# Second chunk of the gated convolution input, DFT tables of the channels and first transfers in a two-layer encoder kernel on one Trainium2 core

## The chip, the core and the metric

The kernel runs on one core of a Trainium2 chip. TensorE (PE) multiplies matrices, VectorE (DVE), ScalarE (ACT) and GpSimd (POOL) work on tiles of 128 partitions, SyncE (SP) issues most transfers between the chip's memory and the core's. Each engine works through its own list of instructions in order and waits on semaphores for the others. The metric is the device time of one execution in microseconds; less is better. The time of the kernel before is 1168.14 us, the median of three runs (1167.82 to 1168.42).

## The reference

A trunk of two layers is applied with the same weights to a prompt of 512 positions and to a sample of 1024, both of width 1024, in fp32.

```
even layer:  h = rms_norm(x);  p = h @ w_in
             a_val, a_glu, f_in, a_z, f_z = split(p, five times 512)
             a = a_val * sigmoid(a_glu)
             a = depthwise conv of width 31 (a) + b
             a = silu(layer_norm(a)) * silu(a_z)
             f = Re(DFT over positions and over the 128 channels of each of 4 groups)(f_in)
             f = (f @ w_four per group) * silu(f_z)
             x = x + concat(a, f) @ w_out
odd layer:   u, b, c, z = split(rms_norm(x) @ w_in, four times 1024)
             x = x + (b * conv of width 3 (c * u) * silu(z)) @ w_out
output:      rms_norm(x)
```

## The kernel before

Activations are kept transposed: a tile has 128 channels on the partitions and a chunk of 512 positions along the free axis. The prompt, Q in the code, is one chunk; the sample, S, is two. A projection makes one output tile of 128 channels and 512 positions in PSUM. Its precision comes from splitting: each weight half and each activation is cast to fp32r (`hi`) on ScalarE, and the remainder (`lo`) is taken by a subtraction on VectorE or GpSimd. A projection then is three times eight matmuls over the eight tiles k of the width: `hi*hi`, `hi*lo`, `lo*hi` (`project`, line 175). In the trace the activations are `nh` and `nl` (normed), `rh` and `rl` (the prompt's, normed late), the weights `wo`, or `wp` where they lie in other buffers.

`load_w` (line 152) brings two halves of 256 KB through SP's queue into four raw buffers `wf`, casts them on ScalarE and subtracts on GpSimd. Weight tiles go to four buffers `wo`, or into a named pool: `load_w(..., "F")` takes four of the 16 buffers `F`, which also hold the inputs `x` of a chunk, eight tiles, and the tables `tb` of the position DFT, split into `tbh` and `tbl`.

The norm of a sample chunk (`norm_in`, `norm_in_rest`) sums squares, has PE transpose the sum (`cs`), computes the reciprocal root with a Newton iteration on GpSimd (`y`, line 214), makes a diagonal `d` on ScalarE (line 223) and spreads it with a matmul by ones (`r`, line 262). Then VectorE multiplies each of the eight `x` by `r`, ScalarE casts `nh`, and VectorE, for two of the eight GpSimd, subtracts `nl`.

The program is written out in order at lines 1130 to 1212; a scheduler then moves instructions of each engine by a timeline of its own, within the data dependences. The even layer's first part runs: the prompt's gated values (`l1_glu(Q)`), its Fourier input, the sample's first norm, the prompt's Fourier transform, its gates, the sample's second norm, then the sample's gated values `l1_glu(S, skew=True)`. For each of four channel tiles j that function makes the gate `glu` (sigmoid, tile `sig`) and the value `val` on both chunks and multiplies them into `a`. For j = 0 the order is gate and value on chunk 0, then `between`, which is the prompt's last Fourier gate `fz` with its weights in `F`, then gate and value on chunk 1. For j = 1 to 3 the gate runs on both chunks, then the value.

`fourier_tables` (line 446) loads and splits the position tables and multiplies the channel DFT `cdft` with the four group matrices `wf4`: two fp32 matmuls `wcs`, for the prompt and again, with another scale, for the sample. Beside all this VectorE runs the convolutions of width 31 (`conv31`, line 567), 30 taps of a multiply and add for each channel tile: `cv`, 128x512 for the prompt, 128x1024 for the sample.

The first lines of the program issue the small parameters `par_sb` and the constants `cst_sb` on ScalarE's queue, and the prompt's `x` and the first weights on SP's.

Of the kernel before, what the change touches and what calls it, by code (L numbers as in the profile page):

```python
# [11 lines left out]
AF = mybir.ActivationFunctionType  # L12
# [4 lines left out]
P = 128  # L17
# [46 lines left out]
def encoder(ctx: ExitStack, tc: tile.TileContext, xp, xs, w1, w1o, w2, w2o, wf4, par, cst, cdft, dft, outp, outs):  # L64
    nc = tc.nc
# [278 lines left out]
    def l1_glu(seq, h, skew=False, w0=None, between=None):  # L344
        for j in range(4):
            if seq is S:
                a = dp("a", seq.T + 2 * HALO)
            else:
                a = pool.tile([P, seq.T + 2 * HALO], F32, name=nm("ap"), tag="ap", bufs=4)
            nc.vector.memset(a[:, 0:HALO], 0.0)  # L350
            nc.vector.memset(a[:, HALO + seq.T:], 0.0)
            sig = [None] * seq.nc

            def do_glu(c, pq=None):
                if pq is None:
                    pq = project("glu", wg, h[c])
                t = sig[c] = pg("T", "sig")
                act_scaled(seq, t, pq, AF.Sigmoid)
                if seq.r is not None:
                    tt(t, t, seq.r, ALU.mult)  # L360

            def do_val(c, pq=None):
                if pq is None:
                    pq = project("val", wv, h[c])
                tt(a[:, HALO + c * CH:HALO + (c + 1) * CH], pq, sig[c], ALU.mult)

            if j == 0 and w0 is not None:
                pg_, pv_ = project_pair(w0, h[0])
                do_glu(0, pg_)
                do_val(0, pv_)  # L370
                seq.a.append(a)
                continue
            wg = load_w(w1, 4 + j)
            if skew and j == 0:
                wv = load_w(w1, j)
                for c in range(seq.nc):
                    do_glu(c)
                    do_val(c)
                    if c == 0 and between:
                        between()  # L380
            else:
                for c in range(seq.nc):
                    do_glu(c)
                wv = load_w(w1, j)
                for c in range(seq.nc):
                    do_val(c)
            seq.a.append(a)
# [51 lines left out]
    def azs(seq, h, c, js, n):  # L439
# [3 lines left out]
            l1_az(seq, h, c, [j])  # L443
        yield 1

    def fourier_tables(seq):
        seq.tab = {}
        for part in range(seq.parts):
            for q in range(2):
                t = ld("tb", dft[2 * part + q])  # L450
                seq.tab[q, part] = split(t, "F", "tb")
        wf4_sb = ld("w4", wf4)
        base = 0 if seq is S else 2 * P
        chan_dft = ld("cd", cdft)
        seq.wcs = []
        for q in range(2):
            pw = ps_st("wcs")
            nc.tensor.matmul(pw, chan_dft[:, base + q * P:base + (q + 1) * P], wf4_sb, start=True, stop=True)
            t = pg("T", "wcs")
            nc.scalar.copy(t, pw)  # L460
            seq.wcs.append(t)

    def fourier(seq):
# [663 lines left out]
        return t  # L1127


    nc.scalar.dma_start(par_sb, par)  # L1130
    xq = load_x(Q, 0, range(0, 1))
    w0 = load_w_pair(w1, 4, 0, lambda: xq.extend(load_x(Q, 0, range(1, 4))))
    xq += load_x(Q, 0, range(4, KD))
    one = pg("T", "one")
    nc.vector.memset(one, 1.0)
    nc.vector.tensor_copy(ones_r, one[:, 0:P])
    nc.vector.tensor_scalar(out=lnmean, in0=one[:, 0:P], scalar1=1.0 / 512.0, scalar2=None, op0=ALU.mult)
    nc.scalar.dma_start(cst_sb, cst)
    hq, hi_i, lo_i = norm_late(Q, xq)
    hq = [hq]  # L1140
    norm_late_r(Q, xq, hi_i, lo_i)
# [54 lines left out]
    at, seq = [], []  # L1196
# [80 lines left out]
```

## Time and profile before

| what | value |
|---|---|
| median of the runs | 1168.14 us |
| profiled execution, its own time | 1167.41 us |
| its span, first to last instruction | 1165.6 us |
| mean granted clock of TensorE | 0.991 |
| PE busy | 1135.6 us, 97% |
| DVE busy | 864.1 us, 74% |
| ACT busy | 470.9 us, 40% |
| POOL busy | 539.3 us, 46% |

Times in the trace are microseconds from the span's start. A row of a timeline gives start, duration, engine, line, operation, tiles, shape and count, and in brackets the idle time of the engine just before, with what ended it. The ends of matmuls are modelled and overlap; the starts are the measure of pace. A row of waits gives the waiting instruction and what it waited for, the sum in us, the number of times and the longest.

### The profile page before, as it was taken

The numbers are of one execution on the slowest core, as the hardware profiler recorded it, in microseconds if no ns is written. First come the engines' busy times: TensorE is split into PE (matmuls) and PEld (weight loads), VectorE is DVE, ScalarE is ACT, GpSimd is POOL, SyncE is SP. The second block draws the span as 40 slices with busy tenths as digits, with TensorE's granted clock in tenths as the row PEclk, the third lists the DMA queues.
The fourth block names the chain that finished last, engine by engine and source line by source line (L and its number), as shares of the span: only waits on it lengthen the run. The fifth ranks groups of instructions, "written<-read, shape, count | busy, mean of one in ns | idle before, by whom it ended". The sixth has DMA issues, their size and how long they took to land. (4 is left out here: it accounts for less than half of the span.)

```text
span 1165.6 us, 15047 instructions
## 1 busy us (share of the span) xinstructions
PE 1135.6 (97%) x5208; PEld 936.4 (80%) x5208; DVE 864.1 (74%) x1202; ACT 470.9 (40%) x823; POOL 539.3 (46%) x448
## 2 busy tenths in 40 slices
PE   7999989999999999999999999999999999999995
PEld 6778868888888888887778887878888888888895
DVE  5899988999899995678775799886464546554565
ACT  6543552233233344445433544442433333343431
POOL 3453632222246565544645454645545454444551
PEclk9999999999999999999999999999999999999998
DMA  9423312111234656535634758644222122034853
GB/s 325 138 91 95 104 46 64 55 37 55 82 97 153 205 190 223 172 99 183 192 123 145 283 191 297 224 157 142 89 75 79 58 82 82 28 106 141 281 173 123
DMA packets 89212, 159.63 MB, mean 137 GB/s; under 512 B 9904, under 2 KB 13488, under 8 KB 89136
## 3 DMA queue, kind: packets, MB, share of 16 engines
q1 hardware_dynamic: 88848, 158.37, 41.2%
q8 instruction: 41, 0.67, 0.2%
q14 instruction: 35, 0.29, 0.1%
q10 hardware_dynamic: 288, 0.30, 0.1%
HBM read 127.96 MB, written 30.67 MB: 136 GB/s over the span
## 5 line engine op out<-in xcount | busy, mean ns | idle before, releaser
L146 POOL TENSOR_TENSOR wo<-wf,wo 128x512 fp32r<-128x512 f32 x272 | 377.8, 1406 | 447.6 <-ACT wo L145 330.9
L145 ACT CAST wo<-wf 128x512 fp32r<-128x512 f32 x274 | 160.4, 618 | 217.1 <-PE X L742 37.3
L146 POOL TENSOR_TENSOR wo<-as,wo 128x512 fp32r<-128x512 f32 x80 | 111.3, 1391 | 112.6 <-ACT wo L145 108.1
L564 DVE SCALAR_TENSOR_TENSOR cv<-a,par_sb,cv 128x1024 f32<-128x1024 f32 x120 | 154.3, 1286 | 6.9 <-ACT cv L562 4.6
L189 PE MATMUL one<-ysh,wo 128*128 128x512 f32 x432 | 110.1, 392 | 0.7 <-ACT wo L145 0.4
L145 ACT CAST wo<-as 128x512 fp32r<-128x512 f32 x80 | 49.7, 621 | 140.3 <-PE X L742 86.5
L189 PE MATMUL one<-nh,wo 128*128 128x512 f32 x384 | 93.9, 391 | 2.4 <-ACT wo L145 2.4
L189 PEld LDWEIGHTS one<-ysh,wo 128*128 128x128 f32 x432 | 80.6, 188 | 18.6 <-ACT wo L145 0.9
L110 DVE TENSOR_TENSOR acc<-acc,sq 128x512 f32<-128x512 f32 (+1 forms) x77 | 76.3, 999 | 23.2 <-ACT sq L281 22.5
L564 DVE SCALAR_TENSOR_TENSOR cv<-ap,par_sb,cv 128x512 f32<-128x512 f32 x120 | 90.2, 752 | 2.6
L189 PEld LDWEIGHTS one<-nh,wo 128*128 128x128 f32 x384 | 71.8, 188 | 18.3 <-ACT wo L145 3.2
L742 PE MATMUL X<-bsh,wo 128*128 128x512 f32 x256 | 84.6, 391 | 0.0
L189 PE MATMUL one<-ysl,wo 128*128 128x512 f32 x216 | 58.3, 390 | 0.7 <-DVE ysl L110 0.7
L742 PEld LDWEIGHTS X<-bsh,wo 128*128 128x128 f32 x256 | 48.1, 188 | 10.6
L742 PE MATMUL X<-bsl,wo 128*128 128x512 f32 x128 | 50.1, 391 | 0.0
L189 PE MATMUL one<-nl,wo 128*128 128x512 f32 x192 | 49.3, 392 | 0.0
L189 PEld LDWEIGHTS one<-ysl,wo 128*128 128x128 f32 x216 | 40.5, 188 | 9.9 <-DVE ysl L110 1.1
L110 DVE TENSOR_TENSOR mc<-Z,mc 128x512 f32<-128x512 f32 x16 | 11.1, 691 | 46.9 <-PE Z L742 46.9
L742 PE MATMUL Z<-bsh,wo 128*128 128x512 f32 x128 | 44.3, 389 | 0.0
L742 PE MATMUL X<-ysh,wo 128*128 128x512 f32 x128 | 42.7, 398 | 0.1
L742 PE MATMUL Y<-bh,wo 128*128 128x512 f32 x128 | 42.4, 392 | 0.0
L189 PEld LDWEIGHTS one<-nl,wo 128*128 128x128 f32 x192 | 36.0, 188 | 7.9 <-issue 0.5
(314 smaller groups left out, 2476.3 us busy)
## 6 DMA issues: line engine op xcount, KB each, us to landing
wf<-w SPq DMA_DIRECT2D x224, 256.0 KB, 2.9
wf<-w2o SPq DMA_DIRECT2D x48, 256.0 KB, 3.5
wf<-w1o SPq DMA_DIRECT2D x32, 256.0 KB, 3.1
x1d<-xr SPq DMA_DIRECT2D x24, 256.0 KB, 2.1
x1r<-x1d SPq DMA_DIRECT2D x24, 256.0 KB, 4.0
xr<-x1d SPq DMA_DIRECT2D x19, 256.0 KB, 4.4
x<-xs SPq DMA_DIRECT2D x16, 256.0 KB, 5.3
y<-y SPq DMA_DIRECT2D x16, 256.0 KB, 4.0
```

The lines of the kernel that those rows point to most:

```text
L110: ins = eng.tensor_tensor(out=out, in0=a, in1=b, op=op)
L145: nc.scalar.copy(hi, t)
L146: eng.tensor_tensor(out=lo, in0=t, in1=hi.bitcast(F32), op=ALU.subtract)
L189: nc.tensor.matmul(out[:, 0:width], a[k], act[k][b][:, cols], start=(n == 0), stop=(n == 3 * KD - 1))
L564: nc.vector.scalar_tensor_tensor(out=acc, in0=src[:, t:t + n], scalar=col(w0 + t), in1=acc, op0=ALU.mult, op1=ALU.add)
L742: nc.tensor.matmul(out, self.w[p][a][:, k * P:(k + 1) * P], self.ops[p][k][b], start=(first and n == 0), stop=(n == 11), skip_group_check= ...
```

## The change

Three edits. In `l1_glu` for the sample the gate of j = 1 on chunk 0 runs ahead of `between`, with its weights in `F`; chunk 1 of j = 0 then follows, and for j = 1 only the gate on chunk 1 and the two values are left. In `fourier_tables` the sample no longer multiplies its channel tables: the prompt's two are stored to memory, loaded again and scaled by a constant. At the start a copy of one column from a constant tile stands ahead of ScalarE's first work on data, and the transfer of `cst` moves from ScalarE's queue to SP's, behind the prompt's `x`.

```diff
+            if skew and j == 1:
+                wg = ahead[0]
+                do_glu(1)
+                wv = load_w(w1, j)
+                sig[0] = ahead[1]
+                for c in range(seq.nc):
+                    do_val(c)
+                seq.a.append(a)
+                continue
             wg = load_w(w1, 4 + j)
             if skew and j == 0:
                 wv = load_w(w1, j)
-                for c in range(seq.nc):
-                    do_glu(c)
-                    do_val(c)
-                    if c == 0 and between:
-                        between()
+                do_glu(0)
+                do_val(0)
+                wn = load_w(w1, 5, "F")
+                t = pg("T", "sig")
+                act_scaled(seq, t, project("glu", wn, h[0]), AF.Sigmoid)
+                ahead = wn, t
+                between()
+                do_glu(1)
+                do_val(1)
...
+    wcs_far = []
...
+        if seq is S:
+            seq.wcs = []
+            for q in range(2):
+                t = pg("T", "wcs")
+                nc.sync.dma_start(t, wcs_far[q])
+                nc.scalar.activation(t, t, AF.Copy, scale=math.sqrt(Q.T / S.T))
+                seq.wcs.append(t)
+            return
         wf4_sb = ld("w4", wf4)
-        base = 0 if seq is S else 2 * P
         chan_dft = ld("cd", cdft)
         seq.wcs = []
         for q in range(2):
             pw = ps_st("wcs")
-            nc.tensor.matmul(pw, chan_dft[:, base + q * P:base + (q + 1) * P], wf4_sb, start=True, stop=True)
+            nc.tensor.matmul(pw, chan_dft[:, (2 + q) * P:(3 + q) * P], wf4_sb, start=True, stop=True)
             t = pg("T", "wcs")
             nc.scalar.copy(t, pw)
+            wcs_far.append(park(t, "wcs"))
             seq.wcs.append(t)
...
+    one = pg("T", "one")
+    nc.vector.memset(one, 1.0)
     nc.scalar.dma_start(par_sb, par)
+    nc.scalar.copy(sm("warm")[:, 0:1], one[:, 0:1])
...
-    one = pg("T", "one")
-    nc.vector.memset(one, 1.0)
...
-    nc.scalar.dma_start(cst_sb, cst)
+    nc.sync.dma_start(cst_sb, cst)
```

The scheduler's new timeline moves instructions in the first two fifths of the program; behind that each engine's row is the same. Three places matter here. The first is on PE, where `r` of the sample's second norm stands, before and then now.

```order
L189 MATMUL fz_1419<-rl_134,wp_1408 128x512
L189 MATMUL fz_1419<-rl_138,wp_1408 128x512
L262 MATMUL r_1211<-d_1167,ones_r 128x512
L189 MATMUL fz_1419<-rl_142,wp_1408 128x512
L189 MATMUL fz_1419<-rh_113,wp_1409 128x512
```

```order
L189 MATMUL glu_1426<-nh_784,wp_1416 128x512
L189 MATMUL glu_1426<-nh_789,wp_1416 128x512
L262 MATMUL r_1217<-d_1173,ones_r 128x512
L189 MATMUL glu_1426<-nh_794,wp_1416 128x512
L189 MATMUL fz_1464<-rh_115,wp_1452 128x512
```

Before, `r` came after 15 of the 24 matmuls of `fz`; now it comes after 23 of the 24 of the gate j = 1 on chunk 0, and all of `fz` follows it.

The second place is on PE where the second chunk begins, before and then now; `glu_1448` and `glu_1493` are the gate of j = 0, `val` its value, `glu_1549` the gate of j = 1.

```order
L189 MATMUL fz_1419<-rh_137,wp_1410 128x512
L189 MATMUL fz_1419<-rh_141,wp_1410 128x512
L458 MATMUL wcs_1916<-w_368_1912,cd_1914 128x512
L189 MATMUL glu_1448<-nh_1214,wo_1334 128x512
L189 MATMUL val_1475<-nh_1214,wo_1344 128x512
L189 MATMUL glu_1448<-nh_1219,wo_1334 128x512
L189 MATMUL val_1475<-nh_1219,wo_1344 128x512
```

```order
L189 MATMUL fz_1464<-rh_139,wp_1455 128x512
L189 MATMUL fz_1464<-rh_143,wp_1455 128x512
L189 MATMUL glu_1493<-nh_1220,wo_1340 128x512
L189 MATMUL val_1520<-nh_1220,wo_1350 128x512
L189 MATMUL glu_1549<-nh_1220,wp_1413 128x512
L189 MATMUL glu_1493<-nh_1225,wo_1340 128x512
L189 MATMUL val_1520<-nh_1225,wo_1350 128x512
L189 MATMUL glu_1549<-nh_1225,wp_1413 128x512
```

The matmul `wcs` is gone, and each normed tile `nh` is now used by three matmuls in a row where it was used by two.

The third place is on DVE ahead of the eight products `x` with `r`, before and then now. `cs` is the transposed sum of squares, `cv` a tap of the prompt's convolution, `tbl` a split of a position table, `a` the product of value and gate; in the new file the taps' line is L587.

```order
L110 TENSOR_TENSOR tbl_1897<-tb_1894,tbh_1896 128x512
L564 SCALAR_TENSOR_TENSOR cv_2299<-ap_331,par_sb,cv_2299 128x512 x2
L210 TENSOR_SCALAR y_1151<-cs_1146 128x4
L564 SCALAR_TENSOR_TENSOR cv_2299<-ap_331,par_sb,cv_2299 128x512
L211 TENSOR_SCALAR y_1151<-y_1151 128x4
L564 SCALAR_TENSOR_TENSOR cv_2299<-ap_331,par_sb,cv_2299 128x512 x7
L110 TENSOR_TENSOR a_1331<-val_1381,sig_1379 128x512
L564 SCALAR_TENSOR_TENSOR cv_2299<-ap_331,par_sb,cv_2299 128x512 x5
L286 SCALAR_TENSOR_TENSOR x_1107<-x_1107,par_sb,r_1211 128x512
```

```order
L110 TENSOR_TENSOR fz_1333<-fz_1308,rq_195 128x512
L587 SCALAR_TENSOR_TENSOR cv_2301<-ap_333,par_sb,cv_2301 128x512 x5
L210 TENSOR_SCALAR y_1157<-cs_1152 128x4
L587 SCALAR_TENSOR_TENSOR cv_2301<-ap_333,par_sb,cv_2301 128x512
L211 TENSOR_SCALAR y_1157<-y_1157 128x4
L587 SCALAR_TENSOR_TENSOR cv_2301<-ap_333,par_sb,cv_2301 128x512 x7
L110 TENSOR_TENSOR a_1337<-val_1387,sig_1385 128x512
L587 SCALAR_TENSOR_TENSOR cv_2301<-ap_333,par_sb,cv_2301 128x512 x7
L286 SCALAR_TENSOR_TENSOR x_1113<-x_1113,par_sb,r_1217 128x512
```

The table splits `tbl` have left the row ahead of `y` (all four now stand behind the `x`), and two taps more stand between `a` and the first `x`. On POOL two weight subtractions `wp` more stand ahead of the Newton steps `y`, and on SP the four loads `xr` of the prompt's residual stand behind two weight tiles more.

## Rows read from the trace of the kernel before

**Rows 1.** Waits of PE over the whole execution: engine, tile and line that waited, what for; us in total, times, longest.

```profile
PE pa L199 <- ACT wo L145: 6.5, 1, 6.5
...
PE glu L189 <- DVE nl L110: 2.1, 2, 1.2
...
PE glu L189 <- ACT nh L116: 1.2, 1, 1.2
```

**Rows 2.** Timeline of PE from the last value tile of the sample's first chunk, j = 0, to the first value tile of j = 1.

```profile
147.16 1.98 PE L189 MATMUL fz<-rh,wp 128*128 128x512 f32 x8
...
150.56 1.02 PE L262 MATMUL r<-d,ones_r 128*128 128x512 f32 x2
...
153.52 1.02 PE L458 MATMUL wcs<-w,cd 128*128 128x512 f32 x2
...
155.78 0.50 PE L189 MATMUL glu<-nh,wo 128*128 128x512 f32 x1 [1.24 <-ACT nh L116]
...
162.97 0.51 PE L189 MATMUL glu<-nl,wo 128*128 128x512 f32 x1 [1.19 <-DVE nl L110]
...
164.66 0.50 PE L189 MATMUL glu<-nl,wo 128*128 128x512 f32 x1 [0.95 <-DVE nl L110]
...
184.21 1.07 PE L189 MATMUL val<-nh,wo 128*128 128x512 f32 x4
```

**Rows 3.** Busy time of each engine by stretch: start and end, its length, then busy us and instructions of PE, weight loads, DVE, ACT, POOL, the granted clock, the share of the transfer engines and GB/s.

```profile
160.00:190.00 30.00, 27.87 (x112) 21.78 (x112) 26.42 (x36) 9.96 (x15) 11.00 (x8) 0.94 0.28 88
190.00:260.00 70.00, 70.00 (x314) 58.02 (x313) 63.20 (x70) 19.87 (x35) 18.63 (x26) 1.00 0.14 46
```

**Rows 4.** Timeline of PE in a stretch without gaps, with a broadcast `r` among the matmuls.

```profile
416.84 1.98 PE L189 MATMUL az<-nh,wo 128*128 128x512 f32 x8
...
424.10 1.53 PE L189 MATMUL az<-nl,wo 128*128 128x512 f32 x6
425.46 1.02 PE L262 MATMUL r<-d,ones_r 128*128 128x512 f32 x2
...
426.79 3.82 PE L189 MATMUL az<-nh,wo 128*128 128x512 f32 x16
```

**Rows 5.** Timeline of DVE around the sample's second norm.

```profile
150.51 3.91 DVE L564 SCALAR_TENSOR_TENSOR cv<-ap,par_sb,cv 128x512 f32<-128x512 f32 x5
...
154.33 5.35 DVE L286 SCALAR_TENSOR_TENSOR x<-x,par_sb,r 128x512 f32<-128x512 f32 x8
...
162.24 4.77 DVE L110 TENSOR_TENSOR nl<-x,nh 128x512 fp32r<-128x512 f32 x6
```

**Rows 6.** Timeline of POOL and ACT in the same norm: a weight split, the first Newton step, the diagonal, the casts.

```profile
139.91 1.75 POOL L146 TENSOR_TENSOR wp<-wf,wp 128x512 fp32r<-128x512 f32 x1
...
144.62 0.19 POOL L214 TENSOR_SCALAR y<-y 128x4 int32<-128x4 int32 x1 [1.25 <-DVE y L211]
...
148.21 1.28 ACT L223 ACTIVATE d<-cst_sb,y 128x128 f32<-128x128 f32 x4 [5.70 <-POOL y L110]
...
155.11 5.28 ACT L116 CAST nh<-x 128x512 fp32r<-128x512 f32 x8 [1.70 <-DVE x L286]
```

**Rows 7.** Timeline rows of two additions of DVE, without and with a weight split on POOL beside them.

```profile
122.91 0.68 DVE L110 TENSOR_TENSOR acc<-acc,sq 128x512 f32<-128x512 f32 x1
126.15 1.78 DVE L110 TENSOR_TENSOR acc<-acc,sq 128x512 f32<-128x512 f32 x1
...
124.72 2.66 POOL L146 TENSOR_TENSOR wo<-wf,wo 128x512 fp32r<-128x512 f32 x2 [8.53 <-ACT sq L281]
```

**Rows 8.** Timeline of the start, all engines.

```profile
1.18 0.90 SPq L141 DMA_DIRECT2D wf<-w  x2
...
3.89 1.28 ACT L316 ACT_TABLE_LOAD   x1 [3.89 <-DMA x<-xp]
...
5.81 0.60 ACT L145 CAST wo<-wf 128x512 fp32r<-128x512 f32 x1
...
6.46 0.79 PE L199 MATMUL pa<-rh,wo 128*128 128x512 f32 x1 [6.46 <-ACT wo L145]
...
9.19 0.63 PE L199 MATMUL pa<-rh,wo 128*128 128x512 f32 x1
...
9.62 0.63 PE L199 MATMUL pb<-rh,wo 128*128 128x512 f32 x1
```

**Rows 9.** The tile view of the raw weights `wf`, the two transfers issued in the first 3 us.

```profile
DMA to landing us min/median/max: 4.0/4.4/4.8
```

**Rows 10.** Timeline of ACT's copies of the prompt's channel tables and of the next weight transfer on SP's queue.

```profile
50.91 1.06 ACT L460 COPY wcs<-wcs 128x512 f32<-128x512 f32 x2
...
53.05 0.33 SPq L141 DMA_DIRECT2D wf<-w  x1
```

**Rows 11.** Busy time of each engine from the second norm to the end of the convolutions, columns as in rows 3.

```profile
155.00:426.00 271.00, 268.09 (x1263) 222.30 (x1263) 249.88 (x297) 94.59 (x163) 107.08 (x107) 0.99 0.30 96
```

**Rows 12.** Waits of DVE in that stretch, columns as in rows 1.

```profile
DVE a L110 <- PE val L189: 3.0, 3, 1.1
DVE a L110 <- ACT wo L145: 2.8, 1, 2.8
```

**Rows 13.** Timeline of PE and of DVE at the start of the second layer: the first matmul of its projections and the last subtractions of its normed input.

```profile
439.51 0.39 PE L189 MATMUL one<-nh,wo 128*128 128x512 f32 x1
...
441.36 1.18 DVE L110 TENSOR_TENSOR nl<-x1r,nh 128x512 fp32r<-128x512 f32 x1 [0.52 <-issue]
```

## Prediction

> **What bounds the kernel now.** I read the waits of TensorE first. They sum to little, because PE is busy 97% of the span; but three entries lie where this change works [rows 1]: 6.5 us before the first matmul, which ends with a cast of a weight on ScalarE, and 2.1 us and 1.2 us before `glu` matmuls, which end with the normed tiles `nl` and `nh`. The second view is the timeline of PE around those `glu` waits [rows 2]. From 147.16, where the last value tile of the sample's first chunk is through, to 184.21, where the first value tile of j = 1 begins, PE has 37.05 us. Inside lie three gaps (1.24, 1.19, 0.95 us), but also matmuls that stand further apart than they must: between 155.78 and 162.97 PE takes one k at a time, as the norm hands them over. The third view, busy time by stretch, shows the granted clock at 0.94 from 160 to 190, where the stretch behind has 1.00 [rows 3]: one short time at the lower of the two levels (1.2 of 2.4 GHz) follows the gaps. Fourth, the pace when nothing is missing: 32 matmuls of 128x512 from 416.84 to 424.10 are 0.227 us each, and a broadcast `r` takes 426.79 - 425.46 less two such matmuls, 0.88 us [rows 4]. By that pace 37.05 us are a good deal too long for what is in them, and that is the first term.
>
> **The gate tile ahead of the second chunk.** Between the two marks both orders do the same 120 matmuls: 24 of `fz`, 48 of gate and value of j = 0 on the second chunk, 48 of the gate of j = 1 on both. With one `r` that is 120 x 0.227 + 0.88 = 28.1 us. The stretch before is 37.05, so at most 8.9 us can go: gaps, single-file matmuls, the slow clock and the two `wcs` matmuls, which ran inside this stretch and go with it.
>
> How much of it goes is a question of when the norm delivers. Before, `r` of the second chunk runs at 150.56; VectorE, which has five taps of the convolution in front, starts the eight products `x` only at 154.33 and has the last at 159.68; ScalarE's casts `nh` follow at 0.66 us each from 155.11 [rows 5, 6]. PE stands at the second chunk from 154.5. Now 24 gate matmuls stand ahead, and `r` is after 23 of them: 147.16 + 23 x 0.227 = 152.4, done 153.3. On VectorE two table splits (0.6 to 1.1 us each) have left the row ahead of `y` and two taps (3.82 / 5 = 0.76 us each) have come in ahead of `x`; so `x` starts within 0.7 us of 154.33 as before. PE comes to the second chunk after the last gate matmul and 24 of `fz`, at 153.3 + 25 x 0.227 = 158.9: 4.4 us later, with the norm where it was. And it now takes three matmuls per k, 0.68 us, where `nh` comes every 0.66. I expect no wait for `nh`. Against it: ScalarE has table casts between the `nh`, the first behind the weight tiles of `fz`. Held to the end of `fz`, about 159.3, ten casts at 0.66 end at 165.9, and PE wants the last at 158.9 + 7 x 0.68 = 163.7: up to 2.2 us.
>
> The `nl` are tighter. After the last `x` (about 159.7) VectorE's row has two taps, six `nl`, three tables and one `fz` up to the last `nl`: 2 x 0.66 + 10 x 0.6 to 0.8 (six `nl` from 162.24 took 4.77 [rows 5]), so 167.0 to 169.0. PE asks for the last pair 42 matmuls after 158.9, at 168.4. That leaves 0 to 0.6 us of waiting. With a VectorE subtraction beside GpSimd the price is another: 1.78 us where an undisturbed one takes 0.68, the GpSimd split running from 124.72 on [rows 7]. The Trainium skill ("GPSIMD Engine Reference", section "1. Specifications") says the two engines share their SBUF interfaces and get in each other's way when the VectorE instruction has two SBUF inputs; the trace agrees (1.78 against 0.68). By that rule two `nl` on GpSimd beside this chain would cost up to 2.2 us, by the range of the rows without it 0.6. I take 0.6 us, and keep 0 and 2.5 as ends. The stage gives 8.9 - 0.6 = 8.3 us, bounds 6.4 and 8.9.
>
> GpSimd has two weight splits more ahead of the Newton steps: before, it stood idle 1.25 us for `y` and began at 144.62, after a split of 1.75 at 139.91 and one product [rows 6]. Two more of 1.75 end at 146.9; Newton takes 3.6 (144.62 to 148.21), the diagonal 1.28 on ScalarE, so it is there at 151.8, and PE wants it at 152.4. This cover is 0.6 us; what the splits lose beyond it is paid in full.
>
> **The tables once.** The two `wcs` matmuls are already in the sum. For them come two stores and two loads of 256 KB and two scalings on ScalarE in place of two copies. The stores wait in SP's queue for ScalarE's copies, which end at 51.97; SP's next weight load goes out at 53.05 anyway [rows 10], cover 1.1 us. The loads stand before two weight loads of `fa` and wait for a buffer; one group of `fa`, 48 matmuls or 10.9 us, is still ahead of those weights. I cost it at 0, up to 0.5 us.
>
> **The head.** Before, `x` landed and only then did ScalarE load its table, 1.28 us from 3.89; the first matmul began at 6.46, as soon as the first weight half was cast, from 5.81 [rows 8]. Now the table is loaded on a constant before `x` arrives. The next thing late is the weight: issued from 1.18, landing after 4.0 to 4.8 us [rows 9], so 5.2 at the earliest; with its cast of 0.6 the first matmul is at about 5.85, 0.6 us sooner. The constants `cst` left the start, 193 KB that shared the transfer engines with it, so it may be more; the second weight half (about 6.4) may hold it to nothing. Bounds 0 and 1.28, value 0.6. The first matmuls stand 0.43 us apart (9.19, 9.62 [rows 8]), the lower clock. The Trainium skill ("TensorE: Matmul & The Clock Gate", "Part 1: The HAM clock gate") says that the window by which the clock rises runs free and does not begin with the kernel. By that rule the rise may stay where it is, and 0.6 us at half pace buy 0.3; no row here shows another phase.
>
> **Sum.** 8.3 + 0.6 = 8.9 us. The profiled execution took 1167.41, the median of the runs is 1168.14, 0.73 more. 1167.41 - 8.9 = 1158.5, and as a median 1168.14 - 8.9 = 1159.2.
>
> **Does it last?** From 155 to 426 VectorE is busy 249.88 of 271 us, all on the convolutions between the projections [rows 11]. If it cannot follow, PE pays later, where the second layer starts: its first matmul at 439.51 needs the normed tiles, whose last subtraction ends at 442.5; PE wants that one seven k later, at 439.51 + 21 x 0.227 = 444.3 [rows 13]. Cover 1.8 us. But 5.8 us of VectorE's waits in this time are for PE in two entries alone, value tiles and the cast behind PE's weights [rows 12]; these shrink as PE comes sooner, and with the head VectorE is 6.4 us ahead. PE is 8.9 ahead: 8.9 - 6.4 - 1.8 = 0.7 us given back by this bound; with the smaller waits for PE that I have not listed, nothing. I take nothing.
>
> **Rivals.**
> *VectorE gives part back* (chance 0.17). For it: 92% busy; in the new order four taps stand among the tiles of that norm. If VectorE gains only half of what PE does, 4.4, the wait is 8.9 - 4.4 - 1.8 = 2.7 us: 1161.9; the case goes from 1161.5 to 1165.8. Against it: the waits for PE, and that in this stretch PE never waited for VectorE.
> *VectorE gives all back* (0.07). If it gains only the head, 0.6, PE loses 8.9 - 0.6 - 1.8 = 6.5: 1165.7 and, with a fall of the clock after such a wait, 1166 to 1168. It needs all those waits to be for something else.
> *Slower* (0.06). The second chunk's `r` now stands behind two more GpSimd splits, whose raw weights must land and be cast first. A delay beyond the 0.6 us cover stops PE with everything behind it. From a delay of 0.6 + 8.9 = 9.5 us it is slower; at 15 us it is 1159.2 + 14.4 = 1173.6. Against it: the transfer engines are idle there and a weight takes about 3 us.
> *Nothing changes in the stage*: PE would have to wait as long at the new place; rows 5 and 6 give no cause, and the case lies in the second.
> *Better* (0.02): the later waits of PE fall away too, under 1157.
>
> Forecast 0.68, own range 1157 to 1161.5. The range 1156.5 to 1164.5 leaves out about 2 in 10. A measurement of this kernel tells 0.2%, 2.3 us, from no change: faster 0.68 + 0.17 + 0.02 = 0.87, same 0.07, slower 0.06.
>
> **What would show it.** PE's waits for `nh` and `nl` at `glu` gone or under 1 us together; the clock at 1.00 there; about 28 us from the first gate matmul on the split-off weights to the first value tile of j = 1; first matmul at about 5.9, table load before 3; no new wait for `nl` at the start of the second layer; `wcs` matmuls half as many. Wrong if PE waits for `r` at the new place, if `x` begins after 156, or if a wait for a VectorE tile stands near 430.

## The result and the profile after

The changed kernel takes 1159.15 us (median of 6 runs, 1155.62 to 1161.61) against 1168.15 us of the kernel before (median of 6 runs, 1165.83 to 1168.60). The ratio is 0.9926, with a 95% interval of 0.9915 to 0.9937. Two more comparisons on other chips gave 0.9912 (0.9898 to 0.9926) and 0.9924 (0.9912 to 0.9937). The prediction was 1159.2. Its profiled execution took 1156.63 us, near the shortest of the runs and 10.78 under the profiled execution before; why one execution can differ from the next by this much is part of what follows.

The page of the changed kernel, its head:

```profile
span 1154.8 us, 15035 instructions
PE 1127.6 (98%) x5204; PEld 931.4 (81%) x5204; DVE 858.6 (74%) x1202; ACT 471.1 (41%) x824; POOL 536.0 (46%) x448
```

The waits of PE over the whole execution, columns as in [rows 1]:

```profile
PE pa L199 <- ACT wo L145: 5.1, 1, 5.1
PE one L189 <- ACT wo L145: 4.4, 3, 1.5
PE r L262 <- DVE d L251: 3.0, 1, 3.0
PE z L496 <- DVE x L286: 1.8, 1, 1.8
PE cs L234 <- DVE acc L110: 1.7, 1, 1.7
...
PE one L189 <- DVE ysl L110: 1.1, 1, 1.1
```

Both `glu` entries of [rows 1], 2.1 and 1.2 us, are gone. The wait ahead of the first matmul is 1.3 us shorter (5.12 against 6.46). The entry of `one` for a weight cast (`one<-ACT wo`), in the second layer, is the one to watch: it was 2.8 us before and is 4.4 now.

The stage around the second norm on PE, which answers to [rows 2]:

```profile
143.83 1.98 PE L189 MATMUL glu<-nh,wp 128*128 128x512 f32 x8
...
149.04 1.02 PE L262 MATMUL r<-d,ones_r 128*128 128x512 f32 x2
...
155.61 0.39 PE L189 MATMUL glu<-nh,wo 128*128 128x512 f32 x1
...
164.90 0.39 PE L189 MATMUL glu<-nl,wp 128*128 128x512 f32 x1
165.40 0.73 PE L189 MATMUL glu<-nl,wo 128*128 128x512 f32 x2
...
172.33 1.98 PE L189 MATMUL val<-nh,wo 128*128 128x512 f32 x8
```

The gate on the split-off weights (`wp`) fills the place where PE had stood. From its first matmul to the first value tile of j = 1 it is 172.33 - 143.83 = 28.50 us; before it was 37.05. The matmul at 155.61 has no bracket: nothing was waited for. Only one small gap is left: 165.40 comes 0.50 after 164.90 where the pace is 0.23, so 0.27 us for a late `nl`.

Busy time by stretch (columns as in [rows 3]), around the first norm's `z` and in the stage:

```profile
86.00:98.00 12.00, 10.97 (x56) 9.27 (x57) 11.89 (x22) 4.60 (x8) 3.94 (x4) 1.00 0.45 140
...
160.00:190.00 30.00, 29.89 (x132) 24.43 (x131) 27.43 (x39) 9.68 (x15) 10.30 (x8) 1.00 0.28 88
```

The granted clock stays at the upper level through the stage, where [rows 3] has 0.94. It does so from 86 to 98 as well, and there the kernel before had a fall:

```profile
86.00:98.00 12.00, 9.96 (x46) 8.41 (x45) 11.96 (x22) 6.37 (x11) 2.50 (x2) 0.86 0.42 132
```

This is the same view of the kernel before. Behind the wait of `Z` it was 0.86 before, from 586 to 598; the changed kernel, 11.3 us ahead at that place, has 1.00 from 575 to 587 and from 586 to 598. Set side by side, the places that both traces share show where the 10.78 us of the two profiled executions come from:

```
place on PE                                  before   changed  ahead by
first matmul                                   6.46      5.12      1.34
z, after its wait of 1.75                     88.53     86.75      1.78
pq, behind the fall of the clock             116.75    113.43      3.32
first of the 120 matmuls of the stage        147.16    143.83      3.33
first value tile of j = 1                    184.21    172.33     11.88
second layer, first matmul                   439.51    427.40     12.11
one, after a wait for a weight               553.87    542.56     11.31
Z, after a wait for ysl                      590.40    579.07     11.33
one, after a wait for ysl                    714.50    702.09     12.41
one, after a wait for a weight               739.72    728.79     10.93
last r                                      1157.21   1146.47     10.74
```

The stage gives 8.55 us and the start 1.78. Two falls of the clock that this execution of the changed kernel did not have give 1.54 (88 to 117) and 1.08 (590 to 714; 1.46 with the longer wait of 0.38 at its end taken out). In the second layer some is given back: 0.80 by 553 and 1.48 by 740.

### The profile page after: what moved, and what is told of

It is laid out like the page before. It is cut to its first block, busy times and chain, and to the rows that moved or that the text cites. A ratio compares the mean times of both kernels' runs of the same rounds, so it can differ in the third digit from the quotient of the medians.

```text
span 1154.8 us, 15035 instructions
## 1 busy us (share of the span) xinstructions
PE 1127.6 (98%) x5204; PEld 931.4 (81%) x5204; DVE 858.6 (74%) x1202; ACT 471.1 (41%) x824; POOL 536.0 (46%) x448
## 5 line engine op out<-in xcount | busy, mean ns | idle before, releaser
L146 POOL TENSOR_TENSOR wo<-wf,wo 128x512 fp32r<-128x512 f32 x270 | 371.9, 1394 | 444.0 <-ACT wo L145 323.5
L587 DVE SCALAR_TENSOR_TENSOR cv<-a,par_sb,cv 128x1024 f32<-128x1024 f32 x120 | 154.3, 1286 | 7.1 <-ACT cv L585 5.1
L587 DVE SCALAR_TENSOR_TENSOR cv<-ap,par_sb,cv 128x512 f32<-128x512 f32 x120 | 90.3, 753 | 3.6 <-ACT cv L585 1.0
L765 PE MATMUL X<-bfh,wo 128*128 128x512 f32 x128 | 42.1, 390 | 0.2 <-DVE mc L110 0.2
```

The lines of the kernel that those rows point to most:

```text
L146: eng.tensor_tensor(out=lo, in0=t, in1=hi.bitcast(F32), op=ALU.subtract)
L587: nc.vector.scalar_tensor_tensor(out=acc, in0=src[:, t:t + n], scalar=col(w0 + t), in1=acc, op0=ALU.mult, op1=ALU.add)
L765: nc.tensor.matmul(out, self.w[p][a][:, k * P:(k + 1) * P], self.ops[p][k][b], start=(first and n == 0), stop=(n == 11), skip_group_check= ...
```

## Experiments

All numbers of a comparison are from one chip, with the kernel before run beside it. Medians are of 4 to 12 runs, those of the kernel before of 11 or 27. A ratio is not taken from the two medians, so it can differ a little from theirs.

**The first edit alone.** The kernel before with the first block of the diff and nothing else, shown in part:

```diff
...
-                for c in range(seq.nc):
-                    do_glu(c)
-                    do_val(c)
-                    if c == 0 and between:
-                        between()
+                do_glu(0)
+                do_val(0)
+                wn = load_w(w1, 5, "F")
+                t = pg("T", "sig")
+                act_scaled(seq, t, project("glu", wn, h[0]), AF.Sigmoid)
+                ahead = wn, t
+                between()
+                do_glu(1)
+                do_val(1)
```

> The kernel before with the first edit alone: the gate tile of j = 1 ahead, tables and start as before. Theory (cover for the second norm): the stage from the first gate matmul on the split-off weights to the first value tile of j = 1 falls from 37.05 us to 28.5 (measured in the changed kernel) plus the two wcs matmuls, which stay, 1.8 us: 30.3. That is 6.7 us of gain, median about 1161.4, or up to 8.3 if the wcs matmuls fill a wait; no wait of PE for nh, under 0.5 us for nl. Rival (falls of the clock): the before profile has three short stretches at the low clock (at 90, 165 and 592 us), the changed one none, and their absence is a large part of the gain; then this edit, which can only remove the one at 165, gives 5 us or less, median above 1163.

Measured: 1162.45 us against 1166.54, ratio 0.9973 (0.9958 to 0.9987). The stage took 175.70 - 144.44 = 31.26 us, 5.8 under that of before. PE in the stage:

```profile
161.52 0.50 PE L189 MATMUL glu<-nh,wo 128*128 128x512 f32 x1 [1.04 <-ACT nh L116]
...
166.46 1.88 PE L471 MATMUL wcs<-w,cd 128*128 128x512 f32 x4
...
175.70 1.98 PE L189 MATMUL val<-nh,wo 128*128 128x512 f32 x8
```

The `wcs` matmuls now stand in a row in which nothing is waited for, so they are paid. And there is a wait for the seventh `nh` that the theory did not have. ScalarE and GpSimd show its cause:

```profile
160.33 0.62 ACT L116 CAST tbh<-tb 128x512 fp32r<-128x512 f32 x1 [2.61 <-POOL nl L110]
160.86 1.13 ACT L116 CAST nh<-x 128x512 fp32r<-128x512 f32 x2
```

```profile
156.75 3.55 POOL L110 TENSOR_TENSOR nl<-x,nh 128x512 fp32r<-128x512 f32 x1 [11.65 <-ACT nh L116]
```

A cast of a position table (`tbh`) stood on ScalarE for GpSimd's `nl`, with the `nh` behind it in the row. That subtraction took 3.55 us. In the changed kernel the same pair is there, and the subtraction took 1.30:

```profile
156.12 1.30 POOL L110 TENSOR_TENSOR nl<-x,nh 128x512 fp32r<-128x512 f32 x1 [10.85 <-ACT nh L116]
```

Counted from the stage's first matmul, VectorE comes to its own subtractions `nl` at 12.22 us here and at 13.82 in the changed kernel, so here they run beside GpSimd's.

So the cover works as the theory has it, at 31.26 where it had 30.3. But in time the theory's gain of 6.7 us lies outside the interval (1.5 to 4.9 us), and the rival's 5 or less inside; the median fell by 4.1. The next run shows how both hold.

**The second edit alone.** The tables computed once, with the old order in the stage, shown in part:

```diff
...
+        if seq is S:
+            seq.wcs = []
+            for q in range(2):
+                t = pg("T", "wcs")
+                nc.sync.dma_start(t, wcs_far[q])
+                nc.scalar.activation(t, t, AF.Copy, scale=math.sqrt(Q.T / S.T))
...
```

> The kernel before with the second edit alone: channel tables parked, loaded and scaled. Theory: PE has two matmuls less (1.8 us) ahead of a wait for nh, so the wait grows by as much as the matmuls shrink; 0 to 0.5 us of gain, median 1167.6 to 1168.2, and the wait of PE for nh at the second chunk is 2.5 to 3 us in place of 1.2. Rival: the tables were on the path; 1.8 us of gain, median 1166.3.

Measured: 1166.67 against 1166.54, ratio 1.0005 (0.9992 to 1.0018). PE's waits in it:

```profile
PE glu L189 <- DVE nl L110: 2.6, 2, 1.7
PE glu L189 <- ACT nh L116: 2.1, 1, 2.1
```

Against [rows 1] the wait for `nh` grew from 1.2 to 2.1 us (the theory had 2.5 to 3) and that for `nl` from 2.1 to 2.6. The timeline of PE shows what that means:

```profile
147.65 1.98 PE L189 MATMUL fz<-rh,wp 128*128 128x512 f32 x8
...
163.46 0.50 PE L189 MATMUL glu<-nl,wo 128*128 128x512 f32 x1 [1.67 <-DVE nl L110]
...
183.18 1.98 PE L189 MATMUL val<-nh,wo 128*128 128x512 f32 x8
```

The first `nl` comes 163.46 - 147.65 = 15.81 us behind the stage's first matmul, and in [rows 2], with the tables' matmuls, 162.97 - 147.16 = 15.81 as well. The matmuls had been lying beside a wait, and without them PE waits. Removed alone they bring nothing; removed together with the wait they count. The two edits together say the same, below.

The whole stage is nevertheless shorter here, 183.18 - 147.65 = 35.53 us against 37.05. Behind the second wait for `nl` the rest of it takes 18.03 us here and 19.55 before. The 1.52 us between them are a fall of the clock that came at another place; the clock is the third number from the end. Here and then before:

```profile
155.00:160.00 5.00, 3.72 (x9) 2.73 (x10) 5.00 (x8) 4.11 (x7) 1.29 (x1) 0.66 0.00 0
165.00:170.00 5.00, 4.86 (x20) 3.77 (x21) 4.89 (x9) 1.60 (x3) 0.00 (x0) 1.00 0.00 0
```

```profile
165.00:170.00 5.00, 5.00 (x16) 3.83 (x15) 4.89 (x8) 0.55 (x2) 0.00 (x0) 0.66 0.05 19
```

In this execution the slow stretch lies between the two waits, where the norm sets the pace, and costs nothing; before, it lies behind them and is paid. Against this old stage the first edit alone gains 35.53 - 31.26 = 4.27 us, which is what its median gained.

**The third edit alone.**

```diff
+    one = pg("T", "one")
+    nc.vector.memset(one, 1.0)
     nc.scalar.dma_start(par_sb, par)
+    nc.scalar.copy(sm("warm")[:, 0:1], one[:, 0:1])
...
-    nc.scalar.dma_start(cst_sb, cst)
+    nc.sync.dma_start(cst_sb, cst)
```

> The kernel before with the third edit alone: table load on a constant, cst moved to SP's queue. The prediction's term: first matmul at 5.85, gain 0.6 us, median 1167.5. By the changed kernel's trace the first matmul is at 5.12 (1.34 us earlier), the clock is up at 8.8 in place of 11.7, and z at 86.75 in place of 88.53: gain 1.8 us, median 1166.3. Rival (given back): VectorE or GpSimd set the pace behind, and the gain is gone by the second norm: median 1168.1.

Measured: 1165.46 against 1166.54, ratio 0.9995 (0.9986 to 1.0004). The first matmul is at 5.27, near the changed kernel's 5.12. By the interval the edit lies between a loss of 0.5 and a gain of 1.6 us, by the medians it gains 1.1; so the prediction's 0.6 and no gain both fit, and the 1.8 read from two profiles does not.

**The first two edits, without the third**, on two chips.

> The changed kernel without its third edit (start as before). If the edits add up, the changed kernel's 9.0 us less the head's 1.8 is 7.2: median 1160.9. By the prediction's terms 8.3: median 1159.8. Rival: the head brings nothing that lasts, 9.0: median 1159.2.

> The changed kernel without its third edit, now beside the changed kernel on one chip (on another chip it had a ratio of 0.994 to the kernel before). Theory (the start lasts, though not wholly): 0.5 to 1.5 us above the changed kernel. Rival 1 (given back in the second layer): the same, within 0.3 us. Rival 2 (the earlier first matmul also saves the slow matmuls up to the clock's rise): 2 to 3 us above.

Measured: ratios of 0.9940 (0.9925 to 0.9955; 1159.20 against 1166.54) and 0.9934 (0.9922 to 0.9946; 1159.12 against 1167.30). Beside the second one the changed kernel ran on the same chip, 1157.78:

> The changed kernel a third time, as the mark for the three runs beside it. So far a ratio of 0.9926 and 0.9912 to the kernel before: 0.991 to 0.993 expected.

Its ratio was 0.9924 (0.9912 to 0.9937). So the third edit is worth 1.3 us by the medians, which is the theory's 0.5 to 1.5; but the intervals overlap, and no gain is not excluded. The first two edits are worth 7.3 and 8.2 us by the medians, where the first alone had 4.1 and the second nothing. Their stage in the first of these runs took 176.15 - 147.63 = 28.52 us, as in the changed kernel; against the old stage's 35.53 to 37.05 that is 7.0 to 8.5 us, which takes in both medians. The 7.3 is near what adding up the profiles had given (7.2), the 8.2 near the prediction's terms (8.3); the two chips do not decide between them.

**The changed kernel again, and VectorE's load.** The next three ran on one chip. The first is the changed kernel itself. The others leave out or repeat 8 of the 120 taps of the prompt's convolution, so they compute another one; VectorE runs it between the projections up to the second layer:

```diff
-        for t in range(1, width):
+        for t in range(1, width - 2 if (width == CK and n == CH) else width):
```

```diff
+        more = [1, 2] if (width == CK and n == CH) else []
-        for t in range(1, width):
+        for t in list(range(1, width)) + more:
```

> The changed kernel itself again, on the chip of the runs below. In the first comparison it took 1159.15 us against 1168.15; on another chip the kernel before took 1166.54 and the changed kernel without the third edit 1159.2. Theory A (the start's 1.3 us is given back in the second layer, where PE waits for weights casts behind VectorE's tiles): 1159.0 to 1160, a ratio of 0.993 to 0.995, the same as without the third edit (0.994). Rival B (the start lasts): 1157.5 to 1158.3, a ratio of 0.9925 or under.

> The changed kernel with 8 of the 120 taps of the prompt's convolution left out (the last two of each of the four channel groups; the output is another): 8 x 0.76 = 6.1 us less for VectorE before 430 us. Theory (the cover for VectorE is not used up): no change of the time beyond 0.5 us, PE's row up to 430 us the same. Rival (VectorE gives part back): if VectorE's lag is what PE waits for at 542, 549, 702 and 729 us (1.39, 1.47, 1.09, 1.52 us in the changed kernel's profile), these waits shrink to those of before or under, and the median falls by 1 to 3 us.

> The changed kernel with 8 taps more in the prompt's convolution (two of each channel group done twice; the output is another): 6.1 us more for VectorE before 430 us. In the changed kernel's profile the last nl of the second layer's input ends at 429.6 and PE asks for it at 427.4 + 21 x 0.227 = 432.2, a cover of 2.6. Theory: 6.1 - 2.6 = 3.5 us of wait at that place, less what VectorE's own waits in the stretch take up (it is idle about 7 of 170 us from 260 to 430): 0 to 3.5 us, median 1159 to 1163. By the prediction's cover (nothing left) all of it is paid: 6 us, median 1165 or more.

Measured: the changed kernel 1157.95 against 1167.95, ratio 0.9912 (0.9898 to 0.9926); with 8 taps less 1158.38, ratio 0.9912 (0.9899 to 0.9925); with 8 taps more 1158.47, ratio 0.9921 (0.9909 to 0.9933). Theory A of the first, that the start is given back, expected 0.993 or more and is not borne out; the ratio lies where rival B had it.

Six microseconds of VectorE less bring nothing, and six more cost 0.5 us, within the interval. With the taps more, the last subtraction for the second layer on VectorE starts at 436.36 and PE begins that layer at 429.39:

```profile
429.39 0.39 PE L189 MATMUL one<-nh,wo 128*128 128x512 f32 x1
```

```profile
436.36 0.68 DVE L110 TENSOR_TENSOR nl<-x1r,nh 128x512 fp32r<-128x512 f32 x1
```

The last `nl` is 7.7 us behind PE's first matmul there, in the changed kernel 2.2 (428.49 + 1.14 - 427.40), and yet PE has no wait of over 0.3 us at this place. The order of the matmuls was made anew with the longer row, and takes more matmuls on `nh` first. So the cover at the second layer's start is not a fixed 1.8 us, as the prediction had it.

The waits of the second layer were also supposed to be VectorE's. They did not shrink with the taps left out: 1.39 and 1.53 us near 544 and 551, 1.51 near 731. And they differ between executions of one and the same kernel. The wait of `one` for a weight near 729, in the changed kernel's first profile, and in those of the two repetitions:

```profile
728.79 2.11 PE L189 MATMUL one<-ysh,wo 128*128 128x512 f32 x8 [1.52 <-ACT wo L145]
```

```profile
731.00 2.11 PE L189 MATMUL one<-ysh,wo 128*128 128x512 f32 x8 [0.35 <-ACT wo L145]
```

```profile
729.52 2.11 PE L189 MATMUL one<-ysh,wo 128*128 128x512 f32 x8 [0.49 <-ACT wo L145]
```

So the 1.48 us that the table above has as given back by 740 belong for the most part to that one execution, and not to the change.

**The two halves of the start.** The changed kernel with the transfer of `cst` back on ScalarE's queue:

```diff
-    nc.sync.dma_start(cst_sb, cst)
+    nc.scalar.dma_start(cst_sb, cst)
```

> The changed kernel with the transfer of cst back on ScalarE's queue at the start; the table load on the constant stays. Theory (the table load is what the first matmul waited for): first matmul between 5.1 and 5.5 us as in the changed kernel, same time within 0.5 us. Rival (the 193 KB of cst at the start share the transfer engines, 0.6 us at 315 GB/s): first matmul at 5.7 to 6.0, 0.4 to 0.6 us slower.

Measured: 1158.12, ratio 0.9917 (0.9903 to 0.9931), beside 1157.78 for the changed kernel; first matmul at 5.11. So the early table load brings the first matmul forward. The place of the 193 KB shows only behind it: the second weight half is cast at 6.04, where the changed kernel's three profiles have 5.43 to 5.56. In time the 0.34 us between the medians is within the noise, so a small price, such as the rival's 0.4 to 0.6, is not excluded.

**The same remedy at another place.** In the changed kernel PE's largest wait ahead of the second layer is `z` at 86.75. It needs a buffer that the first norm's `r` holds until VectorE has read it for the last product `x`. With `r` in the pool with four buffers, the order of the instructions has a gate tile `az` there:

```diff
-        return norm_apply(xt, rstd_end(ds)[0], PC_N1, (3, 7) if c else ())
+        if c == 0:
+            r = ps("r")
+            nc.tensor.matmul(r, ones_r.bitcast(F32), ds[0], start=True, stop=True)
+        else:
+            r = rstd_end(ds)[0]
+        return norm_apply(xt, r, PC_N1, (3, 7) if c else ())
```

> The changed kernel with one line more: the broadcast r of the sample's first norm goes to a buffer of the four-deep PSUM pool in place of the two-deep one. There the second z had to wait until the last product x had read r (1.75 us at 86.75); with it in another pool the order has 23 matmuls of a gate tile az ahead of the next z. The same remedy as the change's first edit, at another place. Theory: the waits for x (1.75) and for zl (0.28) go, and with them the fall of the clock at 88 us that three of six profiles show (1.5 to 3 us): median 1.8 to 3.5 us under that of the changed kernel. Rival: VectorE is the bound of the stretch to 430 us, and PE pays at the second norm or at the second layer's start: the same as the changed kernel.

> The kernel x2_r_mm again: the changed kernel with the first norm's r in the four-deep PSUM pool. Beside the changed kernel it was 0.95 us lower with intervals that overlap, and its profile had a wait of 1.07 us for VectorE's x ahead of a gate tile az in place of the 1.75 us at z. Theory: 0.5 to 1.5 us under the changed kernel (0.7 us of wait, and no fall of the clock at 88 us). Rival: the same within 0.3 us.

Measured: 1157.00, ratio 0.9902 (0.9886 to 0.9918), beside 1157.95 for the changed kernel; and on the other chip 1155.24, ratio 0.9897 (0.9885 to 0.9910), beside 1157.78. It is the fastest of all, by 0.95 and 2.54 us, where 1.8 to 3.5 and 0.5 to 1.5 had been expected; neither range holds its number. In the second comparison its interval and the changed kernel's (0.9912 to 0.9937) do not overlap. The wait did not go wholly. The changed kernel, and then this one in its second run:

```profile
86.75 0.71 PE L496 MATMUL z<-wcs,eo 128*128 128x128 f32 x4 [1.75 <-DVE x L286]
```

```profile
86.64 2.11 PE L189 MATMUL az<-rh,wo 128*128 128x512 f32 x8 [1.07 <-DVE x L286]
```

Now a gate tile waits 1.07 us, again until the last `x`, which fits a buffer of the other pool that `r` now holds; that was not tried. What is new is the clock. Of the twelve profiles taken with the 1.75 us wait, or one of 1.1 to 1.8, at `z`, eight show a granted clock of 0.72 or 0.86 from 86 to 98, while the two with the tile in the gap have 1.00:

```profile
86.00:98.00 12.00, 11.36 (x60) 9.78 (x61) 12.00 (x23) 5.67 (x10) 4.31 (x4) 1.00 0.44 151
```

This is the second of the two. Two profiles are few; that the fall never comes there is not shown.

## Why the prediction was right, and where it was not

**The stage was right, at its size.** It was to fall from 37.05 us to 28.1 plus a residual wait of 0.6; it is 28.50, with 0.27 us of waiting, and 28.50 to 28.55 in the five other profiles with both edits in which the taps and `r` are as they were. No wait for `nh`, the clock at 1.00, and the `wcs` matmuls gone with it, as was said. The rows show why, around the norm:

```profile
145.30 1.28 ACT L223 ACTIVATE d<-cst_sb,y 128x128 f32<-128x128 f32 x4 [4.46 <-POOL y L110]
```

```profile
151.72 5.36 DVE L286 SCALAR_TENSOR_TENSOR x<-x,par_sb,r 128x512 f32<-128x512 f32 x8
```

The products `x` begin at 151.72; with the 3.33 us by which everything is earlier here that is 155.05, 0.7 behind the 154.33 of before, the bound that the prediction gave. The cover of `r` was underrated: the diagonal `d` ends at 146.58 and PE asks for `r` at 149.04, which is 2.46 us and not 0.6. The two additional splits had been priced at 1.75 us each, the longer of the rows at hand, from the moment GpSimd was idle before; the two took 2.54 us together. By the table GpSimd's first Newton step is at 141.72, in the old time 145.05, and not 146.9. So a delay had further to go before PE would pay for it than the prediction's slower rival supposed. The 37.05 us are those of an execution that paid for the slow clock; where the fall lies beside the waits the old stage takes 35.53, and the gain there is 7.0 and not 8.55.

**The price of the tables** was right as it was put: nothing of their own, and the two matmuls inside the stage's sum. The experiments make this sharper. Alone this edit brings nothing (by the interval between a gain of 0.9 and a loss of 2.1 us); on top of the first it brings 3.2 us by the medians of one chip (1162.45 and 1159.20). Between the stages of these two runs lie 31.26 - 28.52 = 2.74 us. Of them 1.72 are the `wcs` matmuls that no longer lie beside a wait (by the starts: from 166.46 to the second matmul behind them, at 168.41, it is 1.95 us, one matmul of 0.23 included), and 1.04 are the wait for `nh`. That the wait went is owed to where VectorE's row then lay, and is no price of the tables.

**The start was right by its size, but the steps were not.** The first matmul was to come at 5.85 and came at 5.12, which is 1.34 us earlier than before and more than the bound of 1.28, because the weight half landed earlier, 3.2 us after its issue and not 4.0: its cast starts at 4.46, not 5.2. Why it landed earlier is not shown; with `cst` back on ScalarE's queue it was 3.2 as well.

```profile
1.18 1.28 ACT L1156 ACT_TABLE_LOAD   x1 [1.18 <-PEq L1289]
...
4.46 0.60 ACT L145 CAST wo<-wf 128x512 fp32r<-128x512 f32 x1
...
5.12 0.79 PE L199 MATMUL pa<-rh,wo 128*128 128x512 f32 x1 [5.12 <-ACT wo L145]
...
8.80 0.39 PE L199 MATMUL pa<-rl,wo 128*128 128x512 f32 x1
```

This is the start of the changed kernel; at 8.80 the matmuls begin to follow at 0.23 us in place of 0.43. The first matmul is 0.95 to 1.35 us earlier in the profiles with this edit, but that lead is not the gain. The place where the pace doubles is not tied to the first matmul:

```
kernel                     first matmul   pace doubles   z       z less half of both
before                         6.46          11.74      88.53        79.43
first edit alone               6.40           9.44      87.41        79.49
without the third, second      6.40          12.50      88.83        79.38
changed, first                 5.12           8.80      86.75        79.79
changed, second                5.32          10.55      87.56        79.63
changed, third                 5.24          11.34      87.69        79.40
third edit alone               5.27           9.27      87.15        79.88
```

The last column differs by 0.5 us, while `z` differs by 2.1. That is what half pace means: an earlier first matmul buys half of its lead, and the other half comes only if the pace doubles earlier too. Where the rise comes early the last column is up to 0.4 higher, so there even less is bought. Pairs with a like rise say the same: 87.41 and 87.15 are 0.26 apart, 88.53 and 87.69 are 0.84; with half of the difference between their rises taken out, leads of 1.13 and 1.22 us buy 0.18 and 0.64.

Whether the edit also brings the rise forward, the rows do not show. Over all profiles it stands at 9.44 to 12.50 without the edit (mean 10.69 of five) and at 8.77 to 11.65 with it (mean 10.11 of nine). So the edit is worth about 0.6 us if the rise stays where it is, and about 1.2 if on average it moves along; the runs (1.1 by the medians for the edit alone, 1.3 on top of the others, with the intervals given above) hold both. The prediction had a lead of 0.6 at full price. The lead was twice as long, so if it was bought at half, the number 0.6 came out by luck.

The Trainium skill ("TensorE: Matmul & The Clock Gate", section "Part 1: The HAM clock gate") says that the window by which the clock rises runs free and does not begin with the kernel. The trace of before could not show it; these rows agree, since two executions with the first matmul at 6.40 doubled the pace at 9.44 and at 12.50.

**Falls of the clock outside the stage were not in the sum.** The profiled execution before had two, at 88 and at 592, that the one after had not; they are 1.54 and some 1.5 us. The edits don't touch either place. Behind the wait at `z` near 88 the clock fell in two of the three profiles with the old stage and in six of the nine with the first edit that have this wait. At 592 it fell in two of those three, and in none of the eleven with the first edit; no run shows why, or that it is more than chance. The averages leave little room for such falls: over the runs of one chip the mean granted clock is 0.9923 before (11 runs) and 0.9945 after (6 runs), and at full load that difference of 0.0022 of 1160 us is about 2.6 us, an estimate, of the 10.0 measured there. The stage's own fall, which the sum had, is 0.06 of 30 us by [rows 3], or 1.8 of them. On another chip it is 0.9925 and 0.9934, about 1 us of 9.5. So the two falls are part of why the profiled executions lie 10.78 us apart where the medians lie 9.0, and the medians do not show that they belong in the sum.

**"I take nothing" for VectorE was right, and for a better reason than was given.** The prediction's bound was 0.7 us given back at the second layer's start, 0.17 for a part and 0.07 for all of it. Not even 6.1 us of more work there cost what can be measured. The bound took the order of the matmuls as fixed, and the order goes with the change.

**What stays open.** How often the old stage pays for its fall of the clock is known from three profiles alone: two paid (37.05 and 37.06 us), one did not (35.53). On the chip of the first experiments 4 of 27 executions of the kernel before took 1161.8 to 1162.1 us, 4.5 to 4.8 under the median; none of them was profiled, so what they did without is not known. Nor is it settled what makes the waits for weights in the second layer differ between 0.35 and 1.52 us from one execution to the next; VectorE's load before 430 us is not it.

## What to carry to other kernels

Where PE waits for a norm, look for a tile that doesn't need it, put it ahead, and count what else lies beside the wait: work under a wait brings nothing when it alone is removed, and its full length once the wait is covered, so that edits worth 4 and 0 us alone were worth 7 together. A wait on PE can cost more than its length, since the clock may fall behind it; how often is for many runs to say, not for one profile. At the start of a kernel, half pace halves what an earlier first matmul buys, unless the pace also doubles earlier.

## What the hardware showed that was not expected

The same subtraction on GpSimd, 128x512, took 1.30 us in the changed kernel and 3.55 us with the first edit alone. VectorE beside it, in the second case:

```profile
156.66 0.68 DVE L110 TENSOR_TENSOR nl<-x,nh 128x512 fp32r<-128x512 f32 x1
157.26 0.68 DVE L110 TENSOR_TENSOR tbl<-tb,tbh 128x512 fp32r<-128x512 f32 x1
157.86 1.28 DVE L110 TENSOR_TENSOR nl<-x,nh 128x512 fp32r<-128x512 f32 x2
...
159.66 1.19 DVE L110 TENSOR_TENSOR tbl<-tb,tbh 128x512 fp32r<-128x512 f32 x1
```

VectorE kept its 0.68 us an instruction until the last one, which took 1.19, and GpSimd was stretched, by 2.25 us. The rows before, [rows 7], had it the other way round: there VectorE went to 1.78 us beside a split on GpSimd. Either engine can be the one that loses, and the prediction had priced only VectorE's loss. In the changed kernel the last product `x` and a tap of the convolution ran beside the 1.30 us, and both have one operand in PSUM; VectorE's first `nl` began only behind it, at 157.65. In the five other profiles with both edits and the same order here the subtraction took 1.29 to 1.31 us. The Trainium skill ("GPSIMD Engine Reference", section "1. Specifications") says that the two engines share SBUF interfaces and that an instruction of VectorE with two SBUF inputs contends; the rows agree.

Executions of one kernel differ by up to 6 us (1155.62 to 1161.61), and the profiles name three sources: where the pace doubles at the start (8.80, 10.55 and 11.34 us in three executions of the changed kernel), whether and how long the clock falls behind the wait at `z` (0.72, 0.86 or 1.00 from 86 to 98 in the same three), and the waits for weights near 729 (1.52, 0.35 and 0.49 us in the same three).
